# One recurrent layer and one convolution layer on one core: conditioning products unsplit on four column groups, and scores in half blocks

## The chip, the cores and the metric

The kernel runs on one core of one Trainium2 chip. The metric is the time on the device in microseconds (us); the time shown for a kernel is the median of several runs. A profile is one execution of the same program, recorded by the hardware, and it has its own time. The engines are named as the profile names them: PE (TensorE, matrix products) with PEld (its weight loads), DVE (VectorE), ACT (ScalarE), POOL (GpSimd), and SP, which only issues transfers here.

## The reference

The network has two layers over 512 latent tokens of width 1024, with 256 context tokens beside them. What matters here is the conditioning of the first layer and the recurrence (HGRN2) of the first layer:

```python
def _ada(cvec, w, b):
    m = jax.nn.silu(cvec) @ w + b                      # shift, scale, gate
    return jnp.split(m, 3, axis=-1)

def _modulate(x, g, shift, scale):
    return _rmsnorm(x, g) * (1 + scale) + shift

# per chunk of 16 tokens, 16 heads of 128 channels, both directions
inter  = jnp.einsum('bhck,bhkv->bhcv', qc * jnp.exp(bcum), state)
scores = jnp.einsum('bhtk,bhsk->bhts', qc * jnp.exp(bcum - b_ref), kc * jnp.exp(b_ref - bcum))
intra  = jnp.einsum('bhts,bhsv->bhtv', jnp.where(mask, scores, 0.0), vc)
```

Layer 0: conditioning, modulation of the tokens and of the context, projections to queries, values, two forget gates and an output gate, the recurrence forward and backward, readout, output projection. Layer 1: a convolution module. At the end there is a norm over the width.

## The kernel before, in words

Everything is float32. A large product is made in float32r, which takes one pass on PE: an operand is split into a high part (`hi`, by ACT or POOL) and a rest (`lo`, by DVE or POOL, `split`, lines 134 to 142), and three products are summed. A product that is left in float32 shows as two records of PE, each with a weight load of its own.

**First stage.** `ada_start(jj, ...)` (lines 144 to 166) is called for jj = 0 to 3 and makes shift and scale of two blocks of 128 channels each time. Its weights are four tiles `ada` of 512 KB (128 partitions x 2 x 512). The conditioning vectors (two: latent and context) are the stationary operand with 2 or 4 columns, the weights move, and the sum over the eight pieces of 128 channels stands in 2 or 4 rows of one bank, `adaps`. The table `ADA_SPLIT` says which tiles are split: 12 of the 16, ten with their rest on DVE and two on POOL; the other four are multiplied in float32 (line 150). `adarow` copies the rows to SBUF, and four small products with `sel` (line 161, `adat`) transpose them and add the halves of the split. From these come `mod_s` and `mod_g`, then the modulated tokens `h_hi` and `h_lo` (lines 201 to 203), then `early_products` (lines 248 to 254): five projections, `pe`, that are accumulated while the channels come in, 120 products of 128x512 in all. The stage ends with the last of them. The loads are issued by SP in the order of the program; the tiles `ada` share six buffers.

**Recurrence.** Eight groups of two heads follow. `gla` makes the scores of one head: 512 tokens are four blocks (`NB`) of 128, and in a block there are three levels (`lev` 2, 1, 0: tokens in different halves of 128, in different halves of 64, in different halves of 32) and the two directions inside a chunk of 16, `dg` 0 and 1. Each of the five is a product of 128x128x128 per block into one bank (lines 465 and 471), so 20 float32 products per head, and one `copy_predicated` on DVE per bank takes from it what its mask allows into `a1` or `a2`. POOL adds the two (`h_A`, line 477), and PE multiplies the sum with the values.

**What sets the order.** The program is built by a framework that orders the instructions of all engines with a cost model of its own; only the loads of the first stage keep the order in which they are written. So the products of the next group (`pz`, `pc`, `pq`, `pv`, `pg`) stand between the steps of a head on PE's queue, and an edit in one place can move instructions elsewhere.

Of the kernel before, what the change touches and what calls it, by code (L numbers as in the profile page):

```python
# [9 lines left out]
F32 = mybir.dt.float32  # L10
F32R = mybir.dt.float32r
# [5 lines left out]
P = 128  # L17
# [18 lines left out]
ADA_SPLIT = ((1, 1, 1, 1), (1, 0, 2, 1), (1, 0, 2, 1), (1, 1, 0, 0))  # L36
# [16 lines left out]
C_END = C_TAP + P  # L53
# [7 lines left out]
def hybrid_kernel(ctx: ExitStack, tc: tile.TileContext, xT, ctxT, cvec, consts, norm_g, ada_b, ada_a, ada_c,  # L61
# [63 lines left out]
    sc4 = cpool.tile([P, KD, 4], F32R, name="sc4")  # L125
    V.tensor_copy(out=sc4[:, :, 0:2], in_=sc)
    V.tensor_tensor(out=sc4[:, :, 2:4], in0=sc, in1=sc4[:, :, 0:2].bitcast(F32), op=ALU.subtract)
# [16 lines left out]
    def ada_start(jj, raws, pool, sel):  # L144
        ps = ps_m.tile([P, 512], F32, name=f"adaps{jj}", tag="ms")
        n = 4 if ADA_SPLIT[jj][0] else 2
        for kk, raw in enumerate(raws):
            if not ADA_SPLIT[jj][kk]:
                for k in range(2):
                    mm(ps[0:2], lhsT=sc[:, 2 * kk + k, :], rhs=raw[:, k, :], start=(kk == 0 and k == 0), stop=(kk == 3 and k == 1))  # L150
                continue
            hi, lo = split(pool, raw, [2, 512], f"ada{jj}_{kk}", V if ADA_SPLIT[jj][kk] == 1 else G, ("ahi", "alo"), 2)
            for k in range(2):
                mm(ps[0:4], lhsT=sc4[:, 2 * kk + k, :], rhs=hi[:, k, :], start=(kk == 0 and k == 0), stop=False)
            for k in range(2):
                mm(ps[0:2], lhsT=sc4[:, 2 * kk + k, 0:2], rhs=lo[:, k, :], start=False, stop=(kk == 3 and k == 1))
        row = pool.tile([4, 512], F32, name=f"adarow{jj}", tag="adarow", bufs=2)
        V.tensor_copy(out=row[0:n], in_=ps[0:n])
        pt_ = ps_m.tile([P, 512], F32, name=f"adat{jj}", tag="ms")
        for i in range(4):  # L160
            mm(pt_[:, 2 * i:2 * i + 2], lhsT=row[0:n, i * P:(i + 1) * P], rhs=sel[0:n], start=True, stop=True)
# [49 lines left out]
    with l0:  # L211
# [8 lines left out]
        with tc.tile_pool(name="pinit", bufs=1) as pi:  # L220
            mk = pi.tile([P, 5, P], F32, name="mk")
            eye = pi.tile([4, 4], F32, name="eye")
            nc.gpsimd.dma_start(out=eye, in_=consts[0:4, C_IDN:C_IDN + 4])
            sel = pi.tile([4, 2], F32, name="sel")
            V.tensor_tensor(out=sel, in0=eye[:, 0:2], in1=eye[:, 2:4], op=ALU.add)
# [30 lines left out]
            for jj in range(4):  # L256
                ada_start(jj, araws[jj], pi, sel)
# [71 lines left out]
        def gla(h, j, sg, qs, v):  # L329
# [109 lines left out]
            for lev in (2, 1, 0):  # L439
# [3 lines left out]
                kl = pt.tile([P, L], F32, name=f"{n}_kl{lev}", tag="lk", bufs=2)  # L443
# [4 lines left out]
                else:  # L448
                    ql = pt.tile([P, L], F32, name=f"{n}_ql{lev}", tag="lq", bufs=2)
                    for half in range(2):  # L450
                        dd = [[2 * w, ng_], [CH, hf], [1, CH]]
                        fd = [[2 * hf, ng_], [1, hf], [0, CH]]
                        o, fo = half * w, half * hf + lev * NCH
                        V.tensor_tensor(out=cut(ql, o, dd), in0=cut(qh, o + (1 - half) * L, dd), in1=cut(fac, fo + (1 - half) * 128, fd),
                                        op=ALU.mult)
                        V.tensor_tensor(out=cut(kl, o, dd), in0=cut(kh, o + half * L, dd), in1=cut(fac, 256 + fo + half * 128, fd),
                                        op=ALU.mult)
                p_ = ps_s.tile([P, 512], F32, name=f"{n}_sc{lev}", tag="sc")
                for b in range(NB):
                    bs = slice(b * P, (b + 1) * P)  # L460
                    if lev == 0:
                        qq = cut(qh, L + b * P, [[2 * CH, 4], [CH - L, 2], [1, CH]])
                    else:
                        qq = ql[:, bs]
                    mm(p_[:, bs], lhsT=kl[:, bs], rhs=qq, start=True, stop=True)
                V.copy_predicated(out=cut(a1, 0, [[P, NB], [1, P]]), mask=cut(masks, lev * P, [[0, NB], [1, P]]), data=cut(p_, 0, [[P, NB], [1, P]]))
            for d in range(2):
                p_ = ps_s.tile([P, 512], F32, name=f"{n}_dg{d}", tag="sc")
                for b in range(NB):
                    bs = slice(b * P, (b + 1) * P)  # L470
                    mm(p_[:, bs], lhsT=kh[:, d, bs], rhs=qh[:, d, bs], start=True, stop=True)
                if d == 0:
                    V.copy_predicated(out=cut(a1, 0, [[P, NB], [1, P]]), mask=cut(masks, 3 * P, [[0, NB], [1, P]]), data=cut(p_, 0, [[P, NB], [1, P]]))
                else:
                    V.copy_predicated(out=cut(a2, 0, [[P, NB], [1, P]]), mask=cut(masks, 4 * P, [[0, NB], [1, P]]), data=cut(p_, 0, [[P, NB], [1, P]]))
# [98 lines left out]
        for gi in range(8):  # L574
# [15 lines left out]
            else:  # L590
# [41 lines left out]
                nc.sync.dma_start(out=tap, in_=consts[:, C_TAP:C_END])  # L632
# [221 lines left out]
def _constants():  # L854
# [11 lines left out]
    for i, m in enumerate((far[2] & ~far[1], far[1] & ~far[0], far[0], same & (s <= t), same & (s >= t))):  # L866
        k[:, C_MASK + i * P:C_MASK + (i + 1) * P] = m
# [17 lines left out]
    k[:TAPS, C_TAP:C_TAP + NR] = A.T  # L885
    return k
# [46 lines left out]
```

## Time and profile before

| | us |
|---|---|
| median of 3 runs | 1362.88 |
| lowest and highest | 1358.25, 1363.73 |
| the profiled execution | 1360.55 |
| its span, first to last instruction | 1358.5 |
| PE busy | 1319.3 |
| DVE busy | 947.6 |
| ACT busy | 617.5 |
| POOL busy | 320.1 |

The span is 2.05 us shorter than the time of the same execution. Busy time of PE counts a record from its start to its modelled end, and records of a stream overlap, so the distance from one start to the next is what a record costs in a stream. With n records in one row of the timeline, it is the row's time less the duration of one, divided by n - 1.

### The profile page before, as it was taken

Reading aid. Unit: us, or ns where it says so; the run is one execution under the profiler, and the core shown is the slowest. Engines: PE = TensorE matmul, PEld = TensorE weight load, DVE = VectorE, ACT = ScalarE, POOL = GpSimd, SP = SyncE. Lnnn points to the kernel's source line nnn. Section 1 sums busy time; section 2 is a strip of 40 time slices with the busy share of each in tenths; the row PEclk is TensorE's granted clock in tenths of the full one; section 3 lists DMA queues with packets and bytes.
Section 4 is the critical chain, followed back from the end, with each engine's and each line's share of the span. In section 5 each row is a group of like instructions: output and inputs, shape, how many; then the busy total and the mean of one; then the engine's idle time right before and its main releaser. Section 6 shows DMA issues by size and latency. Waiting matters only on the chain.

```text
span 1358.5 us, 18696 instructions
## 1 busy us (share of the span) xinstructions
PE 1319.3 (97%) x7396; PEld 1112.0 (82%) x7396; DVE 947.6 (70%) x1496; ACT 617.5 (45%) x932; POOL 320.1 (24%) x291
## 2 busy tenths in 40 slices
PE   6999999999999999999999999999999999999997
PEld 2588888998888898899898888986877777788887
DVE  8868787796687877787668868956467566575223
ACT  6455553553345355455255445525323233375331
POOL 3222241240151132132023124204221211122221
PEclk8999999999999999999999999999999999999999
DMA  9312113114112311312312311213424333222221
GB/s 374 120 62 79 47 63 109 63 47 140 62 48 65 122 47 57 115 35 86 128 32 63 109 47 48 62 45 96 146 82 134 110 94 116 78 78 93 93 78 63
DMA packets 36183, 120.15 MB, mean 88 GB/s; under 512 B 4642, under 2 KB 7106, under 8 KB 36096
## 3 DMA queue, kind: packets, MB, share of 16 engines
q1 hardware_dynamic: 35104, 115.79, 26.0%
q0 software_dynamic: 992, 3.18, 1.0%
q8 instruction: 58, 0.95, 0.3%
q14 instruction: 29, 0.24, 0.1%
HBM read 116.85 MB, written 2.10 MB: 88 GB/s over the span
## 4 chain that ended last, share of the span: by engine, by line
PE 63%; DVE 22%; ACT 5%; DMA 4%; issue 3%; POOL 2%; SPq 0%; DVEq 0%; ACTq 0%
PE pa L702 4%; PE pa L701 4%; PE pa L706 4%; PE pz L301 2%; PE pz L302 2%; PE pz L304 2%; PE cop L843 2%; PE cop L847 2%; PE pgt L770 2%; PE cop L844 2%; PE op L530 2%; DVE adacc L176 2%; PE pgt L768 2%; PE op L532 2%; PE pgt L767 2%
## 5 line engine op out<-in xcount | busy, mean ns | idle before, releaser
L701 PE MATMUL pa<-ci_hi,h_hi 128*128 128x512 f32 x256 | 101.3, 407 | 1.9 <-ACT h_hi L649 1.9
L702 PE MATMUL pa<-ci_lo,h_hi 128*128 128x512 f32 x256 | 101.2, 399 | 0.0
L301 PE MATMUL pz<-h_hi,wz_hi 128*128 128x512 f32 x232 | 93.3, 402 | 0.7 <-ACT wz_hi L139 0.7
L116 POOL TENSOR_SCALAR sg<-sg 128x1536 f32<-128x1536 f32 x16 | 76.6, 4786 | 70.0 <-ACT sg L549 69.8
L302 PE MATMUL pz<-h_lo,wz_hi 128*128 128x512 f32 x232 | 92.9, 401 | 0.0
L176 DVE SCALAR_TENSOR_TENSOR adacc<-adb,sc,adacc 128x128 f32<-128x128 f32 x224 | 76.4, 356 | 3.7
L139 ACT ACTIVATE ci_hi<-ci_raw 128x1024 fp32r<-128x1024 f32 x29 | 30.7, 1060 | 105.9 <-PE pa L706 59.3
L141 POOL TENSOR_TENSOR ci_lo<-ci_raw,ci_hi 128x1024 fp32r<-128x1024 f32 x18 | 44.3, 2464 | 132.8 <-ACT ci_hi L139 105.2
L706 PE MATMUL pa<-ci_hi,h_lo 128*128 128x512 f32 x224 | 72.1, 397 | 0.0
L312 PE MATMUL pv<-wv_hi,h_hi 128*128 128x256 f32 x256 | 63.7, 285 | 0.0
L313 PE MATMUL pv<-wv_hi,h_lo 128*128 128x256 f32 x256 | 63.1, 283 | 0.0
L304 PE MATMUL pz<-h_hi,wz_lo 128*128 128x512 f32 x232 | 61.3, 399 | 0.0
L701 PEld LDWEIGHTS pa<-ci_hi,h_hi 128*128 128x128 f32 x256 | 48.7, 190 | 15.1 <-issue 4.1
L432 DVE SCALAR_TENSOR_TENSOR h_S<-h_S,h_dec,h_kb 128x128 f32<-128x128 f32 x96 | 48.8, 508 | 17.5 <-ACT h_kb L426 16.4
L139 ACT ACTIVATE wz_hi<-wz_raw 128x1024 fp32r<-128x1024 f32 x29 | 30.7, 1058 | 66.1 <-DMA wz_raw<-in_w_in 52.8
L302 PE MATMUL pc<-hc,wz_hi 128*128 128x256 f32 x232 | 59.4, 288 | 0.0
L702 PEld LDWEIGHTS pa<-ci_lo,h_hi 128*128 128x128 f32 x256 | 48.7, 190 | 13.0 <-issue 1.4
L301 PE MATMUL pc<-hc,wz_hi 128*128 128x256 f32 x232 | 59.1, 287 | 0.0
L141 DVE TENSOR_TENSOR wz_lo<-wz_raw,wz_hi 128x1024 fp32r<-128x1024 f32 x29 | 35.4, 1222 | 32.5 <-ACT wz_hi L139 32.3
L400 POOL TENSOR_TENSOR h_f<-h_fac 128x16 f32<-128x16 f32 x16 | 10.1, 628 | 198.5 <-DVE h_kl L446 147.4
L843 PE MATMUL cop<-zhi,co_hi 128*128 128x512 f32 (+1 forms) x160 | 54.2, 352 | 0.0
L377 POOL TENSOR_TENSOR h_ref<-h_tot,h_gt 128x64 f32<-128x64 f32 x16 | 17.5, 1091 | 146.4 <-DVE h_ref L404 136.6
(330 smaller groups left out, 4012.1 us busy)
## 6 DMA issues: line engine op xcount, KB each, us to landing
adb<-in_ada_c SPq DMA_DIRECT2D x32, 512.0 KB, 3.5
ci_raw<-in_c_in SPq DMA_DIRECT2D x32, 512.0 KB, 3.4
wz_raw<-in_w_in SPq DMA_DIRECT2D x29, 512.0 KB, 3.4
ada<-in_ada_a SPq DMA_DIRECT2D x16, 512.0 KB, 6.0
wv_raw<-in_w_v SPq DMA_DIRECT2D x16, 512.0 KB, 3.4
wg_raw<-in_w_in SPq DMA_DIRECT2D x16, 512.0 KB, 3.4
cg_raw<-in_c_gate SPq DMA_DIRECT2D x16, 512.0 KB, 3.4
co_raw<-in_c_out SPq DMA_DIRECT2D x16, 512.0 KB, 3.5
```

Source lines behind the costliest of these rows:

```text
L116: (G if pool_min else V).tensor_scalar(out=t, in0=t, scalar1=EMAX, scalar2=None, op0=ALU.min)
L141: lo_eng.tensor_tensor(out=lo, in0=raw, in1=hi.bitcast(F32), op=ALU.subtract)
L176: V.scalar_tensor_tensor(out=acc, in0=raw[:, k, :], scalar=sc[:, k, 0:1], in1=acc, op0=ALU.mult, op1=ALU.add)
L301: mm(ps[:, :T], lhsT=hi[:, k, :], rhs=rhi[k], start=(k == 0), stop=False)
L302: mm(ps[:, :T], lhsT=hi[:, k, :], rhs=rlo[k], start=False, stop=False)
L304: mm(ps[:, :T], lhsT=lo[:, k, :], rhs=rhi[k], start=False, stop=(k == KD - 1))
L312: mm(ps[:, :256], lhsT=lhi[k][:, c], rhs=hi[:, k % 4, :], start=(k == 0), stop=False)
L313: mm(ps[:, :256], lhsT=llo[k][:, c], rhs=hi[:, k % 4, :], start=False, stop=False)
L701: mm(pss[t], lhsT=h_hi[:, 2 * kq + k, c], rhs=hi[:, k, :], start=(kq == 0 and k == 0), stop=False)
L702: mm(pss[t], lhsT=h_hi[:, 2 * kq + k, c], rhs=lo[:, k, :], start=False, stop=False)
L706: mm(pss[t], lhsT=h_lo[:, 2 * kq + k, c], rhs=hi[:, k, :], start=False, stop=(kq == 3 and k == 1))
L843: mm(ps, lhsT=hi[:, i, c], rhs=zhi[ct][:, tok], start=(ct == 0), stop=False)
```

## The change

Two edits, and what follows from them.

1. `ada_start`: no tile is split any more. The stationary operand is `scz`, 32 columns of which two are not zero, and product number c of each four goes to rows 32c to 32c + 31 of the bank `adaps` (column group c of PE's array). `adarow` copies all 128 rows, and the `sel` of the transposing product, now 128 rows with a one in each 32nd row, sums the four groups. `sel` comes from the constants by a small load. The tiles `ada` have eight buffers.
2. `gla`: in heads 0 to 13 the scores are made as products of 64x64, for the two halves of each block, with outputs at rows 0 to 63 and 64 to 127 (two column groups, taken in turn). Level 0 and both directions use the halves on the diagonal, and level 1 too; level 2 uses the halves off it, so that levels 1 and 2 share one bank, `sx`, and one mask. 40 half products per head stand in three banks instead of 20 whole ones in five, and seven `copy_predicated` (six of 64 partitions x 256, one of 128 x 512) instead of five. Heads 14 and 15 keep whole blocks, level 1 ahead of level 2.

```diff
-    def ada_start(jj, raws, pool, sel):
+    def ada_start(jj, raws, pool, scz, sel):
         ps = ps_m.tile([P, 512], F32, name=f"adaps{jj}", tag="ms")
-        n = 4 if ADA_SPLIT[jj][0] else 2
         for kk, raw in enumerate(raws):
-            if not ADA_SPLIT[jj][kk]:
-                for k in range(2):
-                    mm(ps[0:2], lhsT=sc[:, 2 * kk + k, :], rhs=raw[:, k, :], start=(kk == 0 and k == 0), stop=(kk == 3 and k == 1))
-                continue
-            hi, lo = split(pool, raw, [2, 512], f"ada{jj}_{kk}", V if ADA_SPLIT[jj][kk] == 1 else G, ("ahi", "alo"), 2)
             for k in range(2):
-                mm(ps[0:4], lhsT=sc4[:, 2 * kk + k, :], rhs=hi[:, k, :], start=(kk == 0 and k == 0), stop=False)
-            for k in range(2):
-                mm(ps[0:2], lhsT=sc4[:, 2 * kk + k, 0:2], rhs=lo[:, k, :], start=False, stop=(kk == 3 and k == 1))
-        row = pool.tile([4, 512], F32, name=f"adarow{jj}", tag="adarow", bufs=2)
-        V.tensor_copy(out=row[0:n], in_=ps[0:n])
+                c = (2 * kk + k) % 4
+                mm(ps[32 * c:32 * (c + 1)], lhsT=scz[:, 2 * kk + k, :], rhs=raw[:, k, :], start=(kk < 2), stop=(kk >= 2))
+        row = pool.tile([P, 512], F32, name=f"adarow{jj}", tag="adarow", bufs=2)
+        V.tensor_copy(out=row, in_=ps)
...
-                araws.append([pi.tile([P, 2, 512], F32, name=f"ada{jj}_{kk}", tag="araw", bufs=6) for kk in range(4)])
+                araws.append([pi.tile([P, 2, 512], F32, name=f"ada{jj}_{kk}", tag="araw", bufs=8) for kk in range(4)])
...
+            if halves:
...
+                def half_products(out, col, lhs, rhs):
+                    nonlocal first
+                    for b in range(NB):
+                        for i in range(2):
+                            o = b * P + i * HB
+                            c = col(b, i)
+                            got = mm(out[i * HB:(i + 1) * HB, c:c + HB], lhsT=lhs(o), rhs=rhs(b, i), start=True, stop=True)
+                            first = first or got
...
+                    half_products(pz_, lambda b, i: b * HB, lambda o: ops[0][0][:, o:o + HB], lambda b, i: level0_queries(b * P + i * HB, HB))
+                    with tc.issue_after(first.ins):
+                        for d, (t, c0) in enumerate(((pz_, 2 * P), (pd_, 0))):
+                            half_products(t, lambda b, i: c0 + b * HB, lambda o: kh[:, d, o:o + HB],
+                                          lambda b, i: qh[:, d, b * P + i * HB:b * P + (i + 1) * HB])
+                        for lev in (2, 1):
+                            side = (lambda i: 1 - i) if lev == 2 else (lambda i: i)
+                            half_products(px_, lambda b, i: b * P + side(i) * HB, lambda o: ops[lev][0][:, o:o + HB],
+                                          lambda b, i: ops[lev][1][:, b * P + side(i) * HB:b * P + (side(i) + 1) * HB])
+                for acc, t, c0, m in ((a1, pz_, 0, 0), (a1, pz_, 2 * P, 3), (a2, pd_, 0, 4)):
+                    for i in range(2):
+                        r = slice(i * HB, (i + 1) * HB)
+                        V.copy_predicated(out=cut(acc[r], i * HB, [[P, NB], [1, HB]]), mask=cut(masks[r], m * P + i * HB, [[0, NB], [1, HB]]),
+                                          data=cut(t[r], c0, [[HB, NB], [1, HB]]))
+                masked(a1, px_, 0, 1)
```

How the instructions stand before and after the change is shown at three places. The first is PE's queue where the second call of `ada_start` meets the first early products. Before:

```order
L195 MATMUL rx_ss<-rx_sq_233,ones 128x512
L154 MATMUL adaps_280<-ada_0_hi,sc_106 4x512 x2
L156 MATMUL adaps_280<-ada_0_lo,sc_106 2x512 x2
L150 MATMUL adaps_280<-ada_1_152,sc 2x512 x2
L154 MATMUL adaps_280<-ada_2_hi,sc_106 4x512 x2
L251 MATMUL pe_269<-h_hi,we_hi 128x512
L251 MATMUL pe_274<-h_hi,we_hi 128x512
L251 MATMUL pe_279<-h_hi,we_hi 128x512
L156 MATMUL adaps_280<-ada_2_lo,sc_106 2x512 x2
L154 MATMUL adaps_280<-ada_3_hi,sc_106 4x512 x2
```

The same place of the changed program:

```order
L186 MATMUL rx_ss<-rx_sq_207,ones 128x512
L147 MATMUL adaps_254<-ada_0_149,scz 32x512 x2
L147 MATMUL adaps_254<-ada_1_150,scz 32x512 x2
L147 MATMUL adaps_254<-ada_2_151,scz 32x512 x2
L243 MATMUL pe_243<-h_hi,we_hi 128x512
L243 MATMUL pe_248<-h_hi,we_hi 128x512
L243 MATMUL pe_253<-h_hi,we_hi 128x512
L147 MATMUL adaps_254<-ada_3_152,scz 32x512 x2
L244 MATMUL pe_243<-h_lo,we_hi 128x512
L245 MATMUL pe_243<-h_hi,we_lo 128x512
```

Each tile `ada` now has two products of 32 rows, which wait for its load alone; the hi and lo rows, which wait for ACT and DVE, are gone.

The second place is DVE's queue in the same stretch (`ada_lo` is the rest of a split tile, `xn` the normed tokens, `adarow` the copy ahead of the transposing product). Before:

```order
L141 TENSOR_TENSOR we_lo<-we_raw,we_hi 128x1024
L141 TENSOR_TENSOR ada_0_lo<-ada_0_151,ada_0_hi 128x1024
L262 TENSOR_TENSOR xn_255<-x_sb,rx_sq_228 128x512
L262 TENSOR_TENSOR xn_260<-x_sb,rx_sq_228 128x512
L262 TENSOR_TENSOR xn_318<-x_sb,rx_sq_228 128x512
L262 TENSOR_TENSOR xn_323<-x_sb,rx_sq_228 128x512
L285 TENSOR_TENSOR lbe<-lbl 128x32
L202 TENSOR_SCALAR xn_255<-xn_255,mod_g,mod_s 128x512
L202 TENSOR_SCALAR xn_260<-xn_260,mod_g,mod_s 128x512
L203 TENSOR_TENSOR h_lo<-xn_255,h_hi 128x512
L203 TENSOR_TENSOR h_lo<-xn_260,h_hi 128x512
L141 TENSOR_TENSOR ada_3_lo<-ada_3_154,ada_3_hi 128x1024
```

After:

```order
L138 TENSOR_TENSOR we_lo<-we_raw,we_hi 128x1024
L254 TENSOR_TENSOR xn_229<-x_sb,rx_sq_202 128x512
L254 TENSOR_TENSOR xn_234<-x_sb,rx_sq_202 128x512
L254 TENSOR_TENSOR xn_274<-x_sb,rx_sq_202 128x512
L254 TENSOR_TENSOR xn_279<-x_sb,rx_sq_202 128x512
L193 TENSOR_SCALAR xn_229<-xn_229,mod_g,mod_s 128x512
L193 TENSOR_SCALAR xn_234<-xn_234,mod_g,mod_s 128x512
L277 TENSOR_TENSOR lbe<-lbl 128x32
L194 TENSOR_TENSOR h_lo<-xn_229,h_hi 128x512
L149 COPY adarow_263<-adaps_254 128x512
L194 TENSOR_TENSOR h_lo<-xn_234,h_hi 128x512
```

No `ada_lo` stands between `we_lo` and the tokens, and `adarow` of the second call follows the first `h_lo` instead of three more splits.

The third place is the scores of one head in the recurrence (head 8) on PE's queue. Before, the first eight of its 20 products, and a stretch of the next group's `pz` ahead of the others:

```order
L354 MATMUL h_ct<-kc,h_ec 128x128 x4
L465 MATMUL h_sc_6162<-h_ql_6157,h_kl_6156 128x128 x4
L465 MATMUL h_sc_6174<-h_ql_6169,h_kl_6168 128x128 x4
L301 MATMUL pz_00_6445<-h_hi,wz_00_hi 128x512
L302 MATMUL pz_00_6445<-h_lo,wz_00_hi 128x512
```

After, 32 of its 40 half products (the other eight, into `sdb`, stand further down):

```order
L346 MATMUL h_ct<-kc,h_ec 128x128 x4
L475 MATMUL h_s0d<-h_qh,h_kl_6294 64x64 x8
L475 MATMUL h_s0d<-h_qh,h_kh 64x64 x8
L475 MATMUL h_sx<-h_ql_6283,h_kl_6282 64x64 x8
L475 MATMUL h_sx<-h_ql_6289,h_kl_6288 64x64 x2
L356 MATMUL h_s_6215<-v_5823,h_ec 128x128 x2
L356 MATMUL h_s_6219<-v_5823,h_ec 128x128 x2
L475 MATMUL h_sx<-h_ql_6289,h_kl_6288 64x64 x6
```

The half products stand close together, cut here and there by whole products; over the fourteen heads they make 52 unbroken runs on PE's queue. On SP's queue the loads of `wz` and `wv`, which stood among the last `ada` loads, now stand behind them.

## Rows read from the trace of the kernel before

**Rows 1.** The page, parts 1 and 2: busy time, share of the span and instructions of each engine; the span in 40 slices of 34 us, busy tenths of PE.

```profile
PE 1319.3 (97%) x7396; PEld 1112.0 (82%) x7396; DVE 947.6 (70%) x1496; ACT 617.5 (45%) x932; POOL 320.1 (24%) x291
...
PE   6999999999999999999999999999999999999997
```

**Rows 2.** Busy time of each engine by stretch (stretch and its length in us, then busy us and number of instructions of PE, PEld, DVE, ACT and POOL, then granted clock, DMA share, GB/s): first stage in three pieces, recurrence, convolution layer.

```profile
0.00:28.00 28.00, 15.99 (x38) 4.67 (x39) 21.37 (x32) 18.65 (x25) 12.40 (x11) 0.83 0.94 366
28.00:39.50 11.50, 9.06 (x37) 6.04 (x35) 11.50 (x17) 4.96 (x7) 2.86 (x1) 0.98 0.99 396
39.50:75.40 35.90, 35.44 (x148) 22.14 (x148) 26.60 (x58) 15.70 (x28) 6.82 (x8) 1.00 0.15 56
75.40:905.00 829.60, 815.93 (x5211) 731.13 (x5211) 640.15 (x1023) 409.65 (x647) 203.51 (x224) 1.00 0.23 72
905.00:1358.50 453.50, 442.90 (x1967) 348.07 (x1965) 247.95 (x369) 168.53 (x226) 94.53 (x47) 0.99 0.31 96
```

**Rows 3.** The chain of work that ended last, 15 to 42 us (start, us, what).

```profile
10.30 10.07 DMA ada<-in_ada_a
...
20.41 3.38 DVE ada_lo L141
23.78 4.57 DVE xn L262 x4
...
35.48 3.32 DVE ada_lo L141
...
38.91 0.60 DVE adarow L158
...
39.56 1.05 PE adat L161 x8
```

**Rows 4.** Timeline of PE in the first stage (start, us from the first start to the last end, what, number of records): first early products, two records of the second `ada_start` between early products, a transposing product after its wait, an unsplit run of the fourth `ada_start`, the last early product.

```profile
28.09 1.04 PE L251 MATMUL pe<-h_hi,we_hi 128*128 128x512 f32 x3
...
33.86 0.40 PE L252 MATMUL pe<-h_lo,we_hi 128*128 128x512 f32 x1
34.10 0.64 PE L156 MATMUL adaps<-ada_lo,sc 128*2 128x512 f32 x2
34.57 0.39 PE L251 MATMUL pe<-h_hi,we_hi 128*128 128x512 f32 x1
...
39.56 1.05 PE L161 MATMUL adat<-sel,adarow 4*128 4x2 f32 x8 [2.50 <-DVE adarow L158]
...
56.19 3.60 PE L150 MATMUL adaps<-ada,sc 128*2 128x512 f32 x8
...
75.12 0.39 PE L253 MATMUL pe<-h_hi,we_lo 128*128 128x512 f32 x1
```

**Rows 5.** The instructions on the tile `adaps` (number, then ns shortest, median and longest, first and last start in us, shape: stationary rows*columns, then output).

```profile
L154 PEld LDWEIGHTS adaps<-ada_hi,sc x24: 82/85/131, 6.1 to 55.2; 128*4 128x4 f32 x24
L154 PE MATMUL adaps<-ada_hi,sc x24: 390/398/1226, 6.1 to 55.4; 128*4 128x512 f32 x24
...
L150 PE MATMUL adaps<-ada,sc x16: 591/592/1061, 24.4 to 59.2; 128*2 128x512 f32 x16
L158 DVE COPY adarow<-adaps x4: 671/672/678, 12.6 to 62.4; 4x512 f32<-4x512 f32 x4
```

**Rows 6.** The same for the tile `adat`.

```profile
L161 PEld LDWEIGHTS adat<-sel,adarow x32: 181/187/188, 13.4 to 66.3; 4*128 4x128 f32 x32
L161 PE MATMUL adat<-sel,adarow x32: 246/246/267, 13.4 to 66.3; 4*128 4x2 f32 x32
```

**Rows 7.** Timeline of DVE, one row each of the squares of the context (128x256) and of the rest of a token block (128x512).

```profile
44.39 0.68 DVE L203 TENSOR_TENSOR h_lo<-xn,h_hi 128x512 fp32r<-128x512 f32 x1
...
49.20 0.40 DVE L189 TENSOR_TENSOR rc_sq<-rc_sq,rc_sq 128x256 f32<-128x256 f32 x1
```

**Rows 8.** Timeline of ACT at the end of the norm of the tokens.

```profile
21.84 0.63 ACT L197 ACTIVATE rx_sq<-rx_sq 128x512 f32<-128x512 f32 x1
```

**Rows 9.** Timeline of PE and, below it, of PEld at the first scores of a head.

```profile
122.72 1.95 PE L465 MATMUL h_sc<-h_ql,h_kl 128*128 128x128 f32 x16
124.43 0.48 PE L301 MATMUL pz<-h_hi,wz_hi 128*128 128x512 f32 x1
...
122.61 1.87 PEld L465 LDWEIGHTS h_sc<-h_ql,h_kl 128*128 128x128 f32 x16
```

**Rows 10.** The instructions on the scores, tiles `h_sc` (levels) and `h_dg` (directions).

```profile
L465 PEld LDWEIGHTS h_sc<-h_ql,h_kl x256: 188/192/194, 122.6 to 890.0; 128*128 128x128 f32 x128
L465 PE MATMUL h_sc<-h_ql,h_kl x256: 270/275/276, 122.7 to 890.1; 128*128 128x128 f32 x128
...
L466 DVE COPY_PREDICATED a<-masks,h_sc x48: 716/733/754, 127.0 to 891.6; 128x512 f32<-128x512 uint8 x48
...
L471 PE MATMUL h_dg<-h_qh,h_kh x256: 270/275/377, 129.5 to 896.1; 128*128 128x128 f32 x128
```

**Rows 11.** Timeline of PE at a product with one moving column, two records.

```profile
199.09 0.28 PE L178 MATMUL adbps<-ones,adacc 128*128 128x1 f32 x2
```

**Rows 12.** Who waited for whom on PE from 75 to 905 us (us in total, times, longest).

```profile
PE h_o L484 <- POOL h_A L477: 1.3, 2, 0.8
```

**Rows 13.** Timeline of SP: the issues of the last `ada` tiles.

```profile
28.75 3.31 SPq L91 DMA_DIRECT2D ada<-in_ada_a  x2
...
38.83 0.81 SPq L91 DMA_DIRECT2D ada<-in_ada_a  x2
```

More of the change, by code (lines that the diff above doesn't have):

```diff
@@ L35 @@
 ZMIN = -41.0
-ADA_SPLIT = ((1, 1, 1, 1), (1, 0, 2, 1), (1, 0, 2, 1), (1, 1, 0, 0))
 EARLY, EARLY_LOADS, CTX_AT = 5, (3, 2, 0, 0), 2
@@ L52 @@
 C_TAP = C_INV + GRID
-C_END = C_TAP + P
+C_SEL = C_TAP + P
+C_END = C_SEL + 2
 def cut(ap, offset, dims):
@@ L123, in hybrid_kernel @@
     V.tensor_tensor(out=sc, in0=sc, in1=cv, op=ALU.mult)
-    sc4 = cpool.tile([P, KD, 4], F32R, name="sc4")
-    V.tensor_copy(out=sc4[:, :, 0:2], in_=sc)
-    V.tensor_tensor(out=sc4[:, :, 2:4], in0=sc, in1=sc4[:, :, 0:2].bitcast(F32), op=ALU.subtract)
     mod_s = cpool.tile([P, KD, 2], F32, name="mod_s")
@@ L221, in hybrid_kernel @@
             mk = pi.tile([P, 5, P], F32, name="mk")
[L222 to L225, printed above, removed]
+            sel = pi.tile([P, 2], F32, name="sel")
+            nc.gpsimd.dma_start(out=sel, in_=consts[:, C_SEL:C_END])
+            scz = pi.tile([P, KD, 32], F32, name="scz")
+            V.memset(scz, 0.0)
+            V.tensor_copy(out=scz[:, :, 0:2], in_=sc)
             wsrc = [w_in[2, 0, 0], w_in[3, 0, 0], w_in[2, 0, 1], w_in[0, 0, 0], w_in[0, 0, 1]]
@@ L256, in hybrid_kernel @@
             for jj in range(4):
-                ada_start(jj, araws[jj], pi, sel)
+                ada_start(jj, araws[jj], pi, scz, sel)
                 if jj == 0:
@@ L438, in gla, with level_operands @@
             a1, a2 = a1s[h % 2], a2s[0]
-            for lev in (2, 1, 0):
+            halves = h < NH - 2
+            def level_operands(lev):
                 hf = 1 << lev
@@ L442, in gla @@
                 ng_ = L // (2 * w)
-                kl = pt.tile([P, L], F32, name=f"{n}_kl{lev}", tag="lk", bufs=2)
+                kl = pt.tile([P, L], F32, name=f"{n}_kl{lev}", tag="se" if halves and lev == 0 else "lk", bufs=2)
                 if lev == 0:
@@ L447, in gla @@
                                     in1=cut(f16, 0, [[2, ng_], [1, 2], [0, CH]]), op=ALU.mult)
[L448 to L475, printed above, removed]
+                    return kl, None
@@ new lines, in level_operands @@
+                ql = pt.tile([P, L], F32, name=f"{n}_ql{lev}", tag="lq", bufs=2)
+                for half in range(2):
+                    dd = [[2 * w, ng_], [CH, hf], [1, CH]]
+                    fd = [[2 * hf, ng_], [1, hf], [0, CH]]
+                    o, fo = half * w, half * hf + lev * NCH
+                    V.tensor_tensor(out=cut(ql, o, dd), in0=cut(qh, o + (1 - half) * L, dd), in1=cut(fac, fo + (1 - half) * 128, fd),
+                                    op=ALU.mult)
+                    V.tensor_tensor(out=cut(kl, o, dd), in0=cut(kh, o + half * L, dd), in1=cut(fac, 256 + fo + half * 128, fd),
+                                    op=ALU.mult)
@@ L631, in hybrid_kernel @@
                 tap = pt.tile([P, P], F32, name="tap", tag="ec", bufs=1)
-                nc.sync.dma_start(out=tap, in_=consts[:, C_TAP:C_END])
+                nc.sync.dma_start(out=tap, in_=consts[:, C_TAP:C_SEL])
                 for i in range(2):
@@ L865, in _constants @@
     far = [s // w != t // w for w in (64, 32, 16)]
-    for i, m in enumerate((far[2] & ~far[1], far[1] & ~far[0], far[0], same & (s <= t), same & (s >= t))):
+    for i, m in enumerate((far[2] & ~far[1], far[1], far[0], same & (s <= t), same & (s >= t))):
         k[:, C_MASK + i * P:C_MASK + (i + 1) * P] = m
@@ L885, in _constants @@
     k[:TAPS, C_TAP:C_TAP + NR] = A.T
+    for i in range(2):
+        k[i::32, C_SEL + i] = 1.0
     return k
```

28 lines of the change are left out of this document (27 added, 1 removed).

## The prediction

> **What bounds the kernel now.** I read the page first: PE is busy 97% of the span [rows 1]. By stretches there are two regimes. From 75.4 us on PE has work nearly all the time, with 13.7 us idle of 829.6 in the recurrence and 10.6 of 453.5 in the convolution layer [rows 2], while DVE, the next, is busy about three quarters of the recurrence. There what PE is spared comes off the time, and what other engines do counts only where PE waits for it: its waits for the sum of the scores (`h_A`) are 1.3 us in all [rows 12]. The first 75.4 us are different: PE idles 12.0 of the first 28 us and 2.4 of the next 11.5, in which DVE is busy without a break, 11.50 of 11.50 us [rows 2]. The chain of waits says why: after the load it runs over `ada_lo` (3.38 us), four `xn` (4.57) and again `ada_lo` (3.32) on DVE, then `adarow` and the transposing product [rows 3], before which PE stood 2.50 us [rows 4]. From 39.5 to 75.4 PE is full again (35.44 of 35.90, [rows 2]).
>
> **First edit, the conditioning.** What it takes away: 12 splits, so 12 activations on ACT, ten subtractions on DVE and two on POOL. Between 20.4 and 39 us that is 3.4 + 1.2 + 3.4 us of DVE's time, the two long ones because POOL works beside them. What it does to PE: a float32r record of 512 columns costs 0.235 us from start to start (three of them from 33.86 to 34.57), a float32 record (3.60 - 0.59) / 7 = 0.43 [rows 4]. A split tile had four records, 0.94 us, an unsplit one four of 0.43, 1.72. So a call of `ada_start` is 16 records: 16 x 0.43 = 6.9 us if they go one after the other, against 4 x 0.94 = 3.8 (first call), 4.5 (second and third, one tile unsplit) and 5.3 (fourth). If two column groups run at a time it is 3.4 us, with four 1.7. The trace has no two column groups at once, so I take two: the two records of one product use the same group and must follow each other, and if records start in their order, only the second of one product and the first of the next can overlap.
>
> The stage then ends as follows. The 120 early products (28.2 us at 0.235) start at 28.09 and end at 75.5 [rows 4]; in these 47.4 us lie 28.2 + 12.0 of conditioning (half of the second call, the third and the fourth) + 3.1 for three transposing steps of 1.05 + 0.7 for the sum of the context + some 3 of waits, 47. Afterwards the norm is still ready at 22.5 [rows 8]; without `ada_lo` ahead of them the four `xn` take some 2.8 us (0.68 each, the row of a block of that shape, [rows 7]), and PE starts at about 25.5. From there 28.2 + 7.7 (2.25 calls of 3.4) + 3.1 + 0.7 + 2.5 of waits that I keep = 42.2, so the end is at 67.7: **-8 us**. With four groups at once it is -12, with none (2.25 calls of 6.9) 25.5 + 50.0 = 75.5, so 0. The loads allow it: the last `ada` was issued at 38.83 behind waits for buffers [rows 13], and of these there are now eight, with `wz` and `wv` behind them. The copy `adarow` grows from 4 to 128 partitions at the same 512 columns and keeps its 0.67 us [rows 5]; the transposing product keeps its 128 loaded columns [rows 6]. The memset of `scz` and the small load of `sel` lie in the wait for the first tile (PE's first record starts at 6.1, [rows 5]); uncovered they would cost below 1 us.
>
> **Second edit, the scores.** Before, 14 heads x 20 products x 2 records = 560 records at (1.95 - 0.275) / 15 = 0.112 us [rows 9, 10], 62.7 us. Weight loads come at the same distance, (1.87 - 0.19) / 15 = 0.112 [rows 9]: both sides of the array are full. After, 1120 records with 64 moving columns and 64 loaded ones. A float32 record costs 0.43 at 512 columns and 0.112 at 128, so in proportion about 0.058 at 64, an estimate. A load of 128 columns lasts 187 ns and one of 4 columns 85 [rows 5, 6], 0.82 ns a column, so 64 columns are some 53 ns, an estimate too. One after the other that is 1120 x 0.058 = 65.0 us, **+2.3**; with both column groups at work all the time, products and loads, 32.5, **-30.2**. This is the largest unknown: no row shows two groups. Below, -30 is the end, as there are two groups. Above, the row with the strongest warning is the transposing product: with only two moving columns its records still take the time of the loads (the row at 39.56: (1.05 - 0.25) / 7 = 0.114, [rows 4, 6]). No stream of load and product in this trace is denser than that, so the far end is 1120 x 0.112 = 125.4, +62.7. I take the overlap, because loads and products of one group wait on nothing of the other, and the row nearest to a floor, the two records of a one-column product, has them 0.28 - 0.25 = 0.03 us apart [rows 11], which is just what the overlap needs on average (32.5 / 1120 = 0.029).
>
> Where runs of half products meet whole ones, the array may have to empty. The order has 52 runs, so 104 such borders; what a record hides of its 0.275 us behind the next is 0.163 [rows 9, 10], so they cost 0 to 17 us. I take 4, near the lower end, since where the 2-column products of `adaps` stand between 128-column ones, the starts keep their distance (33.86, 34.10, and two records later 34.57, [rows 4]). [...]
>
> The masked copies: five of 0.733 us become six of half the columns (about 0.45, from 0.40 against 0.68 for another operation of these shapes, [rows 7]) and one whole: 3.43 for 3.67 us per head. That changes nothing, since DVE has a quarter of its time free. But all seven follow all the products of a head now, and PE may wait longer for `h_A`; behind the waiting product stand the next projections on PE. For this and for other waits that a faster PE uncovers I take +2 (from 0 to 10 us, the idle time that PE has now in the recurrence being 13.7).
>
> **Sum.** -8 - 30 + 4 + 2 = -32 from 1360.55, so 1328.5; the median of the runs shown is 2.3 us above the profiled execution. I say **1330**.
>
> **Rivals.** (a) The loads do not overlap: products run in two groups, but weights go in through one port. Then the scores cost 65.0 us as one after the other, +2.3, with the borders +6.3; PE is no faster there and uncovers nothing, so the total is 1363 - 8 + 6 = 1361; with free borders 1357. For it speaks that loads and products are now exactly balanced at 0.112 us, so halving one alone gains nothing. (b) A half overlap, say 0.042 us per record: -16 + 4 - 8 + 2, some 1345. (c) Slower: the sequence of load and product has a floor per record, of whatever size. The break-even of the scores alone is 62.7 / 1120 = 0.056 us per record; the whole change, with 8 us from the first stage and 4 for the borders, is slower from 66.7 / 1120 = 0.060 on. At 0.075 they cost 84.0, +21, and the total is 1363 - 8 + 21 + 4 = 1380; at the far end of 0.112, with nothing overlapped, about 1420. For it speaks that nothing in the trace is denser than 0.112 per pair over a stream; against it the single pair at 0.03. [...] (d) The first edit does nothing: the records of 32 rows run singly and the first stage still ends at 75 us. Then, with the overlap of the scores, 1337.
>
> **Chances.** Full overlap with or without some borders, (d) included, 1318 to 1342: 0.48. Half, (b): 0.10. (a): 0.24, of it 0.06 faster and 0.16 the same. (c): 0.15. The rest is scattered. About 0.5%, 6.8 us, is what a measurement of this kernel can tell from no change; so faster 0.64, same 0.18, slower 0.18. The range reaches from the full overlap with four groups in the first stage and free borders (1363 - 12 - 30 = 1321, less some 3 for the runs' spread) over (b) to (a), 1364; it leaves out (c). The likeliest case alone has 1318 to 1342.
>
> **What will show it.** In the profile after: the last early product near 67 us, no DVE-bound stretch ahead of 39 us; 64 records of half products within 1.9 us. If 64 records take 3.7 us, it is (a), and the rows of PEld will have a steady 0.055 us; if more than 4.2 us, (c). If the recurrence has over 25 us of idle PE, my +2 for uncovered waits is wrong. A first stage that ends after 72 us makes the first sum wrong.

## The result and the profile after

The changed kernel takes **1325.86 us** in the median of 4 runs (1325.56 to 1326.18), the kernel before 1363.17 us (4 runs, 1358.25 to 1363.73). The ratio is 0.9735, with a 95% interval of 0.9715 to 0.9754: faster by 2.6%, which is 36 us by the ratio and 37.3 between the medians. I had said 1330.

The page of the changed kernel, parts 1, 2 and 4 (busy time and number of instructions; the 40 slices; the chain by engine), answers to [rows 1]:

```profile
span 1323.5 us, 19786 instructions
...
PE 1288.8 (97%) x7956; PEld 1087.4 (82%) x7956; DVE 934.4 (71%) x1513; ACT 608.2 (46%) x920; POOL 304.3 (23%) x289
...
PE   6999999999999999999999999999999999999997
...
PE 77%; DVE 13%; ACT 4%; DMA 3%; issue 2%; POOL 1%; SPq 0%; DVEq 0%; ACTq 0%
```

PE still bounds the kernel. It has 560 records more than before and 30.5 us less busy time.

The windows of the changed kernel, cut at the first and the last early product and at the last product of the recurrence, answer to [rows 2] (stretch, length, busy us and number on PE, PEld, DVE, ACT, POOL, granted clock, DMA share, GB/s):

```profile
0.00:24.70 24.70, 12.91 (x40) 3.36 (x41) 12.58 (x25) 11.88 (x19) 8.06 (x10) 0.86 0.92 346
24.70:39.50 14.80, 14.17 (x61) 8.04 (x62) 13.76 (x32) 7.55 (x15) 0.00 (x0) 1.00 1.00 386
39.50:69.20 29.70, 27.24 (x123) 19.17 (x121) 16.94 (x38) 8.31 (x14) 7.05 (x8) 0.94 0.21 86
69.20:876.70 807.50, 798.47 (x5789) 710.25 (x5790) 642.66 (x1051) 411.87 (x647) 195.14 (x224) 1.00 0.23 74
876.70:1323.50 446.80, 436.05 (x1947) 346.63 (x1945) 248.48 (x369) 168.57 (x226) 94.06 (x47) 0.99 0.31 98
```

The early products start at 24.7 instead of 28.1 and end at 69.2 instead of 75.5; the recurrence takes 807.5 us, and PE idles 9.0 us in it (13.7 in [rows 2]). The last row is the surprise. The layer behind the recurrence, in which no line was changed, takes 446.8 us; before, counted from the same product, it took 451.2. The same cuts in all traces, from the records' starts and ends, with the two kernels that have one edit each and a second trace of the changed kernel (all described below):

| stage, us | before | first edit | second edit | both | both, once more |
|---|---|---|---|---|---|
| end of the first stage | 75.5 | 68.5 | 79.0 | 69.2 | 68.5 |
| recurrence | 831.8 | 830.0 | 814.9 | 807.6 | 810.1 |
| behind it | 451.2 | 445.4 | 451.1 | 446.8 | 445.5 |
| span | 1358.5 | 1343.9 | 1345.0 | 1323.5 | 1324.1 |

PE in the first stage (timeline: start, time to the last end, what, records, and in brackets the idle time before and who ended it), for [rows 4]:

```profile
41.66 1.05 PE L147 MATMUL adaps<-ada,scz 128*32 128x512 f32 x4
...
47.99 1.92 PE L147 MATMUL adaps<-ada,scz 128*32 128x512 f32 x16 [0.28 <-DVE mod_g L156]
...
54.60 0.95 PE L152 MATMUL adat<-sel,adarow 128*128 128x2 f32 x8
...
59.99 1.43 PE L243 MATMUL pe<-h_hi,we_hi 128*128 128x512 f32 x5 [2.02 <-ACT h_hi L192]
```

A whole call, 16 records, takes 1.92 us: four column groups at once. But PE now runs ahead of what it needs and stands for 2.02 us before 59.99. What DVE did in that time (timeline of DVE):

```profile
55.54 1.58 DVE L193 TENSOR_SCALAR c_sb<-c_sb,mod_g,mod_s 128x256 f32<-128x256 f32 x2
57.04 0.75 DVE L194 TENSOR_TENSOR hc<-c_sb,hc 128x256 fp32r<-128x256 f32 x2
57.71 0.73 DVE L193 TENSOR_SCALAR c_sb<-c_sb,mod_g,mod_s 128x256 f32<-128x256 f32 x2
58.35 0.41 DVE L194 TENSOR_TENSOR hc<-c_sb,hc 128x256 fp32r<-128x256 f32 x1
58.69 0.21 DVE L155 TENSOR_SCALAR mod_s<-adat,ab 128x2 f32<-128x2 f32 x1
58.82 0.27 DVE L156 TENSOR_SCALAR mod_g<-adat,ab,ng 128x2 f32<-128x2 f32 x1
```

The columns of the last call were ready at 54.60 + 0.95 = 55.55, but the context's blocks stand ahead of `mod_s` and `mod_g` in DVE's queue. Behind this wait the granted clock falls to 0.50 (windows of two us, PE's part first, granted clock after the five engines):

```profile
58.00:60.00 2.00, 0.01 (x1) 0.01 (x1) 1.76 (x9) 0.88 (x2) 0.00 (x0) 1.00 0.00 0
60.00:62.00 2.00, 1.89 (x6) 1.31 (x7) 2.00 (x5) 1.63 (x3) 0.00 (x0) 0.88 0.00 0
62.00:64.00 2.00, 2.00 (x6) 1.52 (x6) 1.53 (x4) 0.00 (x0) 0.00 (x0) 0.50 0.00 0
```

From 62 to 64 us PE does six records; at the 0.235 us of [rows 4] it would be eight. In the changed kernel once more PE also waits 2.0 us for `h_hi`, and the granted clock behind it is 0.69, 0.50 and 0.95 from 60 to 66 us, by windows of two. With the first edit alone, with the half products in another order and with halves in all heads (all described below, all with four groups and this order on DVE) PE idles 2.0, 2.0 and 1.8 us between 50 and 60 us, and the granted clock from 60 to 70 is 0.83, 0.83 and 1.00 (0.83 here). In the last of these, where it stays up, the stage ends at 67.9, so most of the loss is the wait itself.

The scores of the first head (timeline of PE) and the rows of the tile `h_sx` (shortest, median, longest ns), for [rows 9, 10]:

```profile
123.49 0.69 PE L475 MATMUL h_s0d<-h_qh,h_kl 128*64 128x64 f32 x16
124.00 0.51 PE L475 MATMUL h_s0d<-h_qh,h_kh 128*64 128x64 f32 x10
124.45 0.55 PE L413 MATMUL h_kt<-kc,h_kb 128*128 128x128 f32 x3
124.92 0.39 PE L475 MATMUL h_s0d<-h_qh,h_kh 128*64 128x64 f32 x5
...
125.15 1.15 PE L475 MATMUL h_sx<-h_ql,h_kl 128*64 128x64 f32 x31
```

```profile
L475 PEld LDWEIGHTS h_sx<-h_ql,h_kl x448: 132/138/138, 125.0 to 779.2; 128*64 128x64 f32 x150
L475 PE MATMUL h_sx<-h_ql,h_kl x448: 222/222/271, 125.1 to 779.3; 128*64 128x64 f32 x150
```

In a stream a half record costs (1.15 - 0.22) / 30 = 0.031 us. The borders show too: the last half record before the transposition starts at 124.00 + 0.51 - 0.22 = 124.29, the transposition at 124.45, 0.16 later; its last record starts at 124.45 + 0.55 - 0.27 = 124.73, the next half record at 124.92, 0.19 later. Over all 52 runs, from the records' starts, the median is 0.205 us into a run and 0.152 out of it.

### The profile page after: what moved, and what is told of

The parts are those of the page before. It is cut to its first block, busy times and chain, and to the rows that moved or that the text cites. A ratio compares the mean times of both kernels' runs of the same rounds, so it can differ in the third digit from the quotient of the medians.

```text
span 1323.5 us, 19786 instructions
## 1 busy us (share of the span) xinstructions
PE 1288.8 (97%) x7956; PEld 1087.4 (82%) x7956; DVE 934.4 (71%) x1513; ACT 608.2 (46%) x920; POOL 304.3 (23%) x289
## 4 chain that ended last, share of the span: by engine, by line
PE 77%; DVE 13%; ACT 4%; DMA 3%; issue 2%; POOL 1%; SPq 0%; DVEq 0%; ACTq 0%
PE pa L734 4%; PE pa L735 4%; PE pa L739 4%; PE pz L293 3%; PE pz L294 3%; PE pz L296 3%; PE op L563 2%; PE cop L876 2%; PE cop L880 2%; PE op L565 2%; PE op L564 2%; PE cop L877 2%; PE pgt L803 2%; PE pgt L801 2%; PE pgt L800 2%; PE py L773 2%
## 5 line engine op out<-in xcount | busy, mean ns | idle before, releaser
L424 DVE SCALAR_TENSOR_TENSOR h_S<-h_S,h_dec,h_kb 128x128 f32<-128x128 f32 x96 | 59.0, 614 | 27.1 <-ACT h_kb L418 26.0
L510 POOL TENSOR_TENSOR h_A<-a,a 128x512 f32<-128x512 f32 x16 | 36.6, 2290 | 129.8 <-DVE a L491 108.0
L369 POOL TENSOR_TENSOR h_ref<-h_tot,h_gt 128x64 f32<-128x64 f32 x16 | 16.8, 1048 | 160.5 <-DVE h_ref L396 157.3
```

## The experiments

Differences in us below are between medians; each ratio is to the runs of the kernel before in the same series.

### Each edit alone

```diff
-            halves = h < NH - 2
+            halves = False
```

> Conditioning of the first layer as in the changed kernel, scores in whole blocks in all sixteen heads. Theory 1 (each edit acts in its own stage, and the layer behind the recurrence gained 4.5 us from the second edit or from where tiles came to lie): last early product near 69.2 us, recurrence 831 us long as before, 1357 us in all (1363.2 - 6.4). Theory 2 (the 4.5 us of the layer behind come with the first edit): the records of pa are 233 ns apart instead of 238 and the time is 1352. Rival (the first edit does nothing by itself): last early product at 75, 1363.

1346.3 us, ratio 0.9879 (0.9864 to 0.9894). That is below every value expected. The first stage ends at 68.5, near the 69.2 of theory 1, but 16 us are gone, not 6: `pa` and `pgt`, and `pz` and `pg` in the recurrence as well, have records 227 ns apart in the median (228 for `pz`), 232 before.

The second kernel has the half scores and, in `ada_start`, the lines of before with `sc4` and the splits.

> Half-block scores in fourteen heads, conditioning split as before. Theory 1 (each edit acts in its own stage): last early product at 75.5 us, recurrence 808 us instead of 832, 1339 us (1363.2 - 24.2); 1334.5 if the 4.5 us of the layer behind come with this edit. Rival (part of the recurrence's gain comes from weights that are ready earlier when the first stage is shorter): recurrence over 812 us, above 1343.

1344.9 us, ratio 0.9871 (0.9854 to 0.9887). The recurrence takes 814.9 us, 16.8 less than before, not 24.2; so the rival's limit is passed, but its reason isn't shown, since records of 512 columns are 232 ns apart here, as before. The end of the first stage, 79.0, is 3.5 us later than before with the same instructions on PE; the granted clock from 40 to 50 us was 0.67 here, with 30 records on PE, and 1.00 before, with 43. So much can its end move with the clock.

### The place of the weights

By the program, the one thing that the first edit changes for the layers behind is that the tile `sc4`, 128 bytes a partition in the pool of constants, is gone, and all tiles allocated behind it, the network's weights among them, lie 128 bytes lower, while `h_hi` and `h_lo` stay. One unused tile of that size puts them back; in the kernel before, it puts them 128 bytes higher. No instruction changes or moves in either.

```diff
+    cpool.tile([P, 32], F32, name="pad")
     mod_s = cpool.tile([P, KD, 2], F32, name="mod_s")
```

> The changed kernel with one tile of 128 bytes a partition, used by nothing, where sc4 stood in the pool of constants: the weight tiles lie where they lay in the kernel before, and no instruction changes or moves. Theory 1 (the records of 512 columns became 5 ns shorter because the weights lie 128 bytes elsewhere against the moving operand): records of pz, pg, pq, pa and pgt again 232 ns apart in the median instead of 227, about 2500 of them, so +11 us, 1337. Rival (the shorter records come with the new conditioning itself, by loads or by the clock): 227 ns and 1326.

> The kernel before with one unused tile of 128 bytes a partition behind sc4, so that the weight tiles lie 128 bytes later; no instruction changes or moves. Theory 1 (what counts is the distance of the weights from the moving operand, and 128 bytes either way give the same): records of 512 columns 227 ns apart instead of 232, about 11 us less, 1352. Rival (only the earlier place helps, or it isn't the place): 232 ns and 1363.

With the pad the changed kernel takes 1335.5 us, ratio 0.9807 (0.9789 to 0.9824), against 0.9735 without: some 10 us more. The kernel before takes 1354.4 with it, ratio 0.9946 (0.9924 to 0.9967): 8 less. Both follow theory 1. The records of `pa` alone, in windows that hold the 768 of them, show it (PE, PEld, DVE). Before:

```profile
930.00:1160.00 230.00, 189.14 (x768) 145.31 (x768) 21.19 (x32) 0.99 0.37 113
```

Before, with the pad:

```profile
930.00:1160.00 230.00, 183.27 (x768) 143.98 (x768) 21.18 (x32) 1.00 0.37 115
```

After:

```profile
900.00:1150.00 250.00, 184.91 (x768) 145.12 (x768) 21.19 (x32) 0.99 0.35 110
```

After, with the pad:

```profile
900.00:1150.00 250.00, 189.12 (x768) 145.25 (x768) 21.18 (x32) 0.99 0.35 110
```

The same 768 records take 189 us with the weights at one place and 183 to 185 at the other. The layer behind the recurrence, from the same product on, takes 451.1 us in the changed kernel with the pad and 445.5 in its second trace without; in the kernel before it takes 443.8 with the pad and 451.2 without, of which some 1.7 us are a stretch at a lower clock (0.55 from 936.2 to 940 us, 10 records against 19).

Sorted, by the addresses of the tiles in the two programs, by the distance in bytes of a record's moving operand from the operand that is loaded for the next record, some 2530 records of 512 columns that lie 128 bytes off a multiple of 256 before are 232.6 ns apart on the mean; after the change some 2360 lie on such a multiple, 227.9 ns apart. In `pz` the network's weights are the loaded operand and `h_hi` moves, in `pa` the weights move and `h_hi` is loaded. Both change alike, so it is the distance that counts and not the place of one operand. By what means it costs time, no run shows.

### How the two column groups overlap

```diff
-                    for b in range(NB):
-                        for i in range(2):
+                    for i in range(2):
+                        for b in range(NB):
```

> The half products of a run in another order: the four of the one column group first, then the four of the other, so that neighbours share the group; operands, results, masks and banks are the same. Theory 1 (the gain is the two groups loading and multiplying at the same time): records of half products 58 ns apart instead of 29, 1120 x 0.029 = +32 us less the few that still change group (one in eight, -4): about 1354 us. Rival (TensorE looks far enough ahead to overlap them anyway, or the gain is that of smaller records): not over 5 us, below 1331. Rival (smaller gain of the pairing, records 42 ns apart): 1340.

1335.0 us, ratio 0.9800 (0.9783 to 0.9817): 9 slower than the changed kernel, far from theory 1 and between the two rivals. The timeline of PE shows why it isn't more:

```profile
125.14 0.27 PE L475 MATMUL h_sx<-h_ql,h_kl 128*64 128x64 f32 x1
125.19 0.22 PE L475 MATMUL h_s0d<-h_qh,h_kh 128*64 128x64 f32 x1
125.25 0.22 PE L475 MATMUL h_sx<-h_ql,h_kl 128*64 128x64 f32 x1
125.25 0.22 PE L475 MATMUL h_s0d<-h_qh,h_kh 128*64 128x64 f32 x1
125.30 0.22 PE L475 MATMUL h_sx<-h_ql,h_kl 128*64 128x64 f32 x1
125.31 0.22 PE L475 MATMUL h_s0d<-h_qh,h_kh 128*64 128x64 f32 x1
125.36 1.32 PE L475 MATMUL h_sx<-h_ql,h_kl 128*64 128x64 f32 x29
```

Within a group records are 0.058 us apart. Where the group changes, the first of the new one (125.14, 125.25, 125.30) run beside the last of the old one, although they stand behind it in the queue, so runs of eight still overlap in part, on the mean (1.32 - 0.22) / 28 = 0.039. From the records' starts, the 1120 half records with the starts of their runs take 66.2 us instead of 54.6. So the gain needs the overlap of the two groups, and a loop order that alternates them is worth 9 us.

### Four groups, two or one in the conditioning

```diff
-                c = (2 * kk + k) % 4
+                c = k
...
```

(with 64 rows in `adarow` and `sel`; for one group c is 0, with 32 rows)

> Conditioning products unsplit on two column groups instead of four (the first block of a tile on one, the second on the other), accumulated over the four tiles, summed by the transposing product over 64 rows. Theory 1 (what I took for the prediction: two at a time, 16 records in 3.4 us): a call with all its tiles there takes 3.4 us instead of 1.9, the first stage ends 2.25 x 1.7 = 3.8 us later than with four, near 73, 1329.5. Rival (since tiles come singly, two groups are as good as four in most calls): below 70.5 us, 1327.

> The conditioning products unsplit, but all on one column group (32 rows), accumulated there over all eight blocks; nothing to sum in the transposing product beyond those 32 rows. Theory 1 (four groups at once are worth it): a call takes 16 x 0.43 = 6.9 us instead of 1.7 to 2.6, the last early product comes at about 76 us instead of 69.2, 1332 us or a little more. Rival (the gain is that the splits have gone from VectorE, the products are hidden in waits): last early product before 71 us, not over 1327.5.

Two groups: 1326.5 us, ratio 0.9742 (0.9729 to 0.9756), as the rival says; in the same series the changed kernel once more, with four:

> The changed kernel as it is, once more, beside the three others on one chip. Both theories: 1326; its profile shows how far the end of the first stage moves from run to run (69.2 us in the first).

1326.7, ratio 0.9743 (0.9730 to 0.9756). One group: 1337.1, ratio 0.9816 (0.9801 to 0.9830), with the end of the first stage at 78.4. PE with two groups:

```profile
48.72 3.63 PE L147 MATMUL adaps<-ada,scz 128*32 128x512 f32 x16
...
57.81 1.05 PE L152 MATMUL adat<-sel,adarow 64*128 64x2 f32 x8
```

and with one:

```profile
40.11 7.05 PE L146 MATMUL adaps<-ada,scz 128*32 128x512 f32 x16
```

With two groups a call takes 3.63 us, the first stage ends at 68.3, and from 24 us on PE waits for nothing before that; with four, the 1.7 us saved per call end in the wait for `mod_g`. With one group the stage ends later than with the split before (75.5). So the first edit lives from the overlap of at least two groups, not from the splits that DVE is spared.

### The context behind the last columns

The context's blocks 2 to 7 are queued on DVE behind the last `mod_g` and the token block 6.

```diff
-CTX_MOD = ((), (), (0, 1, 2, 3, 4, 5), (6, 7))
+CTX_MOD = ((), (), (0, 1), (2, 3, 4, 5, 6, 7))
...
+                    with tc.issue_after(held.ins) if jj == 3 else nullcontext():
+                        modulate(c_sb[:, k, :], k, mod_g[:, k, 1:2], mod_s[:, k, 1:2], hc_hi, hc_lo)
```

> The context blocks 2 to 7 are modulated by VectorE only behind the last conditioning columns and the x block 6, instead of ahead of them. Theory 1 (this wait costs the first stage 2 us of idle PE and then some 2 us at the lower clock): no wait of over 0.7 us for mod_g near 57 us, last early product near 65.5 instead of 69.2, 1322. Rival (PE then waits for the context's tiles or for h_lo instead): last early product and time as before, 1326.

1323.0 us, ratio 0.9708 (0.9689 to 0.9726). The first stage ends at 65.3, as expected, and the granted clock is 1.00 from 56 to 80 us. A second kernel adds to this 128 unused bytes ahead of the tiles behind the weights:

> The changed kernel with the context blocks 2 to 7 behind the last conditioning columns, and 128 unused bytes ahead of the tiles behind the weights, so that zhi and zlo of the last products lie at the distance from the weights at which the other records took 227 ns. Theory 1: the gain of the context's order stays (-2.9 us) and some 250 records of cop become 5 ns shorter, part of cop 90.0 us instead of 91.3; 1321.7 in all. Rival (the place doesn't matter for cop): part of cop 91.3 us, 1323.

1325.5 us, above both values expected, ratio 0.9733 (0.9719 to 0.9746), beside 0.9743 for the changed kernel in that series. The first stage ends at 65.4 again, but of the place nothing is gained: busy time of `cop` falls from 90.85 to 90.64 us, that of `op`, whose moving operand alone has moved, rises from 92.79 to 93.86. So the distance on a multiple of 256 bytes is not the whole rule; for `cop` it did next to nothing, and what decides there stays open. The order of the context saves 3 us of the first stage in two traces out of two; the times, 1 us below the changed kernel in one series and 3 us below it across two, with overlapping intervals, can't settle how much of it arrives.

### Halves in all heads

```diff
-            halves = h < NH - 2
+            halves = True
```

> Half-block scores in all sixteen heads instead of fourteen. Theory 1 (a head gains what the others gained, 16.8 / 14 = 1.2 us by the run with the second edit alone): -2.4 us, 1323.5. Rival (in the last two heads PE waits for the scores' operands or masks anyway, the halves only add borders): no gain, 1326 to 1329.

1345.7 us, ratio 0.9876 (0.9860 to 0.9892): 20 slower, worse than the rival. Who PE waited for from 860 to 912 us, and the windows of the end of the recurrence:

```profile
PE h_o L517 <- POOL h_A L510: 6.4, 2, 3.7
PE wtp L673 <- DMA dw<-in_c_dw: 4.1, 1, 4.1
PE op L563 <- ACT h_ohl L550: 2.1, 1, 2.1
```

```profile
870.00:880.00 10.00, 6.34 (x49) 5.50 (x49) 7.34 (x14) 2.00 (x4) 2.30 (x1) 0.90 0.31 105
880.00:890.00 10.00, 7.44 (x72) 6.37 (x71) 4.99 (x9) 2.54 (x4) 1.82 (x1) 0.76 0.02 4
890.00:900.00 10.00, 7.53 (x35) 6.28 (x35) 1.63 (x3) 2.54 (x4) 0.43 (x1) 0.83 0.05 20
900.00:910.00 10.00, 5.82 (x9) 2.80 (x10) 3.33 (x5) 0.63 (x1) 0.00 (x0) 0.59 0.01 4
```

PE idles 12.9 of these 40 us, and the granted clock falls with it, to 0.59 to 0.90. The longest of its waits, 6.4 us, is for the sum `h_A` behind the masked copies of the last two heads; the other two, for a load and for ACT, stand behind them, and none of the three is among PE's waits there in the changed kernel. In the last two heads no projection of a later head is left to run while the copies and the sum are made; in the fourteen others it hides this wait. That reason is read from the order of the instructions; no run tests it.

### One set of scores in whole blocks

```diff
-                        for d, (t, c0) in enumerate(((pz_, 2 * P), (pd_, 0))):
...
+                        for b in range(NB):
+                            bs = slice(b * P, (b + 1) * P)
+                            mm(pd_[:, bs], lhsT=kh[:, 1, bs], rhs=qh[:, 1, bs], start=True, stop=True)
```

> In the fourteen heads the diagonal product of the second direction (h_sdb) in whole blocks again, with one whole masked copy; 35 runs of half products instead of 52. Theory 1 (a run has a price at its borders: about 0.09 us more at the start and 0.04 more behind the end than beside a whole product, and a slower first pair): the halves of h_sdb cost 8.6 + 1.5 = 10.1 us now, the whole ones 112 x 0.112 = 12.5, so +2.4, 1328. Rival (borders as I took them, 0.04 us each): 224 x 0.029 + 34 x 0.04 = 7.9 against 12.5, +4.7, 1330.5.

1329.0 us, ratio 0.9758 (0.9743 to 0.9773), 2.3 us above the changed kernel in the series: nearer to theory 1, but the intervals overlap, and in the profile the recurrence is 1.4 us shorter and the layer behind it 3.4 us longer (448.9 us against 445.5), where this edit does nothing. The experiment doesn't settle the price of a border; the records of the changed kernel do.

## Why the prediction was right, and where it was not

The time lay 4 us below mine, but two errors of about 10 us each stood against each other in the sum of -32, so that it came so near is luck. With the pad, which takes away the gain that I had not thought of, the changed kernel takes 1335.5 us, 5 above mine; rival (b) had 1345.

**First stage, -8: right in size, by another way.** The stage ends 6.4 us earlier (7.0 in the other two columns of the table that have this edit). I took two groups at a time, because the two records of a product would hold up the others. That was wrong: four run together, 16 records in 1.92 us. For two groups the working was right: 3.63 us per call where I had 3.4, the end at 68.3 where I had 67.7. What I had for four, -12, did not come, since a new wait took it: PE overtakes DVE, stands 2.02 us for `h_hi`, and then has a granted clock of 0.50 from 62 to 64 us. In that case I didn't ask what would be late next. Rival (d) falls: the records don't run singly, and with one group, where they do (16 in 7.05 us, 0.43 apart), the stage ends 3 us later than before. The two long splits that I put down to POOL's work stand beside it in the trace of before (`ada_lo`, 3.38 and 3.40 us, POOL busy in 2.58 and 2.32 us of them); the eight others, with POOL idle, took 1.20 to 1.23, but a `we_lo` of the same shape, beside POOL from end to end, only 1.56. `adarow` takes 0.686 us on 128 partitions, and the loads of the transposing product 192 ns, near the 0.672 us and 187 ns of [rows 5, 6].

**Scores, -30.2: the overlap right.** I took 0.029 us per half record; in a stream it is 0.031, and with both of a pair in one group 0.058, as in rival (a). Both groups share all 128 rows, each load lasts 138 ns, and 31 records with their loads run in 1.15 us, so the loads overlap the running products here, and the worst form of rival (c), with nothing overlapped, falls. The load itself I had read wrongly: 85 ns at 4 columns and 187 at 128 make 134 at 64, not 53. The sum didn't hang on it, since the loads overlap.

**Borders, +4: the step that failed.** I took 4 us of 0 to 17 for the 104 borders; they cost about 13.6. From the records' starts, out of a run it takes 8.2 us for 52 borders (1.5 would be the share of 52 records in a stream), into one 12.5 (8.6 at the mean of a start before, 0.165), and inside, with slower first pairs, 33.8 for 1068 intervals (31.0 at 0.029): 6.7 + 4 + 2.9. The row that I leaned on showed 2-column products among records of 512 columns that keep their distance; half blocks among whole products don't, whatever the width: into a run it takes 0.205 us behind a record of 128 columns (0.109 before) and in most cases 0.41 to 0.43 behind one of 512 (0.234 before), and out of it 0.152 in the median to each. The longer distances make 13.6 / 104 = 0.13 us a border; that the array empties there was my supposition, and no run shows it. All intervals of the scores of the fourteen heads together fell from 73.7 to 54.6 us (15 starts fewer among them), and the recurrence with this edit alone by 16.8. My -30.2 + 4 was 7 to 9 us too much.

**Waits, +2: wrong in sign.** PE idles 9.0 us in the recurrence (11.6 in the second trace), 13.7 before; `h_A` is no longer among PE's waits. The seven copies behind the products, of which I was afraid, cost nothing in the fourteen heads that have a later head's projections behind them, and a good deal in the run with all heads.

**Missing from the sum: the place of the weights, -8 to -10.** I read the removal of `sc4` as work of DVE only. It is as large as the whole first stage, and it is why the layer behind the recurrence gained with no line of it changed. The two runs with the pad, with the same instructions in the same order, show that the distance of PE's two operands counts, by 8 and 10 us.

Together: -7 for the first stage, -17 for the scores, -8 to -10 for the place, 32 to 34 of the 36 us measured. What is left lies within what the runs of one kernel differ by.

## What to carry to other kernels

Small products in two column groups overlapped here, loads included, where neighbours alternate the group: 0.031 us a record instead of 0.058. Gather them in few long runs, since each border to full-width products costs about 0.13 us here. Where an engine gets faster, ask which queue stands ahead of its next operand: four groups gained nothing over two here (the first stage ended at 69.2 and 68.5 us against 68.3) until DVE's order was changed as well (65.3). And if untouched code changes its time, compare where the tiles lie before looking for a cause in the schedule.

## What was not expected of the hardware

- Float32r records of 512 columns come 227 or 232 ns apart in the median, by how far the loaded operand lies from the moving one; 128 unused bytes a partition are worth 8 to 10 us of 1360 here. What decides is not known in full (`cop`).
- Four column groups with two-record float32 products run together: 16 records in 1.92 us, with two groups 3.63, with one 7.05.
- The first records of one group run beside the last of the other although they stand behind them in the queue: three pairs at 125.14 to 125.31.
